# Queueing weight splits behind a tile's norm chain and behind the splits of probabilities in a two-layer hybrid attention trunk

## The chip, the core and the metric

The kernel runs on one core of one Trainium2 chip. The metric is the device time of one execution in microseconds. A core has a matrix engine (TensorE, PE in the profile, with its weight loads as PEld), three engines for elementwise work (VectorE: DVE, ScalarE: ACT, GpSimd: POOL) and a queue that issues the loads (SyncE: SP). Each engine has its own queue, whose order is fixed when the program is built; semaphores order the engines among each other. The program keeps eight PSUM tiles (banks) of 128 x 512 f32, which TensorE writes.

## What is computed

Two layers over 512 tokens of width 1024. Each layer normalizes, projects once, runs eight heads of forgetting attention and eight of dilated windows in parallel, and closes with an output projection and a gated input embedding:

```python
u = rms_norm(h, norm_g)
z = u @ w_in                                   # q, k, v, gate of both kinds, and the forget gate
qa = rms_norm(heads(qa, N_HEADS_FOX), qk_g[0]) # per head, also ka, qb, kb; qb and kb get a partial rope
oa = forgetting_attention(qa, ka, va, log_f) * silu(ga)
ob = dilated_attention(qb, kb, vb) * silu(gb)
h = h + concat([oa, ob]) @ w_out
gate = sigmoid(rms_norm(h, ple_norm_g) @ w_ple_gate)
return h + (p_i @ w_ple) * gate
```

## The kernel before

**Precision.** Every matmul is made of three: each operand is split into a high part, rounded to the fast matmul type (`hi`), and the remainder (`lo`), and hi x hi, hi x lo and lo x hi are added in PSUM (`mm3`). The split of a slab is an ACT copy into `hi` (L157 for weights, L616 for probabilities) and a DVE subtraction into `lo` (L158, L617).

**Weights.** Each pair of heads needs four slabs: `q` in three pieces of 1152, 1152 and 768 columns, and `g` (the gate) of 1024. They are loaded by SP into three raw buffers and split into five slots. `W.pump(n)` splits the next n slabs if a slot is free (`ready`); a slot is free when its earlier slab's last matmul is written. A load for a slab is issued when the third slab ahead of it has been split.

**The steps.** Each layer walks over eight pairs p (0 to 3 dilated, 4 to 7 forgetting). In step p TensorE projects the four token tiles t of pair p (`pj`), computes the scores of pair p-1 (`att_s`), applies the probabilities of pair p-2 to the values head by head (`att_pv`), computes the gate of pair p (`gate_mm`), and transposes the probabilities of pair p-1 (`att_tp` for 64 x 64 blocks into four banks `psS`, `att_tp2` for two whole 128 x 128 blocks per head into one bank `psA`) and the queries and keys of pair p (`att_z`). The matmuls stand in the order of the program (`InOrder`). The other engines' order is made by a scheduler from data dependences and the program's order, so that an instruction that is ready early may be put ahead of one that is written before it.

**The norm chain** of tile t is `evac_proj_a` and `evac_proj_b`: a square on ACT (L431), a reduce and a scaling on DVE (L433, L434), a power on POOL (`f`, L436), the product z on DVE (L449), and for dilated pairs a partial rope (L454 to L457; on DVE for t=3, on POOL otherwise). The value part goes to `V2` (L442, L443). z is the last reader of the projection's bank. There are two banks `psA`; tiles t=0 to 3, the gate and the whole blocks take them in turn.

**The gate** is evacuated by `gate_evac`: a product on DVE that frees the bank (L471), a tanh on ACT (L472), a second product on DVE (L473).

**Probabilities.** `att_pt(j, ...)` splits head j's transposed probabilities into `PT` (hi and lo, 11 blocks each): the two whole blocks into blocks 1 and 2, the rest into 3 to 10. Block 0 is zero. `PT` serves one head at a time, so head 1's split waits until head 0's value matmuls have read it. `att_pv` ends with an ACT copy (`ob`, L633), a DVE sum (L634) and a POOL product with the gate (L636) for each head.

Step p begins with six of eight slices of tile 0, `att_pv` of head 0, `att_pt` of head 1, `W.pump(2)`, the rest of tile 0, three slices of tile 1, `att_pv` of head 1, and then the norm chain of tile 0 (L738 to L746). Two further slabs are pumped after the gate's matmuls (L761).

Of the kernel before, what the change touches and what calls it, by code (L numbers as in the profile page):

```python
# [9 lines left out]
F32 = mybir.dt.float32  # L10
F32R = mybir.dt.float32r
I32 = mybir.dt.int32
AF = mybir.ActivationFunctionType
ALU = mybir.AluOpType
# [3 lines left out]
P = 128  # L18
# [7 lines left out]
HD = 64  # L26
# [175 lines left out]
def trunk(tc, ap):  # L202
# [3 lines left out]
    with ctx:  # L206
# [32 lines left out]
        W = Weights(nc, wp, rp, specs)  # L239
# [28 lines left out]
        QQ = [cp.tile([P, S], F32R, name=f"QQ{i}") for i in range(2)]  # L268
        KK = [cp.tile([P, S], F32R, name=f"KK{i}") for i in range(2)]
        CB = cp.tile([P, S], F32R, name="CB")  # L270
        PT = [cp.tile([P, 11, P], F32R, name=f"PT{i}") for i in range(2)]
        for l in range(DEPTH):
            W.own[("pt", l)] = (QQ, KK)
        C2 = cp.tile([40, S], F32R, name="C2")
# [80 lines left out]
        def rope_tables(l):  # L355
            for kind in range(2):
                for half in range(2):
# [6 lines left out]
                    def g(h):  # L364
# [3 lines left out]
                    V.tensor_tensor(out(Sg), b(nsinT if half == 0 else sinT), g(1 - half),  # L368
                                    op=ALU.mult)


        def square_acc(h, d, E=V):
            if d == 0:
# [52 lines left out]
        def evac_proj_a(l, p, t, ps, st):  # L426
            if p == 0:
                sq = U[t][:, :2 * P].rearrange("p (h d) -> p h d", h=4)
            else:
                sq = tp.tile([P, 4, HD], F32, tag="sq", name="sq", bufs=1)  # L430
            A.activation(sq, ps[:, :2 * P].rearrange("p (h d) -> p h d", h=4), AF.Square)  # L431
            ms = sp.tile([P, 4], F32, tag="ms", name="ms")
            V.tensor_reduce(ms, sq, axis=AX.X, op=ALU.add)  # L433
            V.tensor_scalar(ms, ms, 1.0 / HD, st["E"][:, t:t + 1], op0=ALU.mult, op1=ALU.add)  # L434
            f = sp.tile([P, 4], F32, tag="f", name="f")
            G.tensor_tensor(f, ms, mhalf.to_broadcast([P, 4]), op=ALU.pow)  # L436
            if p == 0:
                V.scalar_tensor_tensor(fx[:, t], ps[:, QW:QW0], st["r"][:, t:t + 1], bf[:, l],
                                       op0=ALU.mult, op1=ALU.add)
            v2 = V2[p % 2]  # L440
            vps = ps[:, 2 * P:QW].rearrange("p (h d) -> p h d", h=2)
            A.activation(v2[:, t, :, 0:HD], vps, AF.Copy, scale=st["r"][:, t:t + 1])  # L442
            V.scalar_tensor_tensor(v2[:, t, :, HD:P], vps, st["r"][:, t:t + 1],  # L443
                                   v2[:, t, :, 0:HD].bitcast(F32), op0=ALU.mult, op1=ALU.subtract)
            return f

        def evac_proj_b(l, p, t, ps, f):
            z = zp.tile([P, 4, HD], F32, tag="z", name="z")
            V.tensor_tensor(z, ps[:, :2 * P].rearrange("p (h d) -> p h d", h=4),  # L449
                            f[:, :, None].to_broadcast([P, 4, HD]), op=ALU.mult)  # L450
            if p < NDIL:
                E = V if t == NT - 1 or p == 0 else G
                tm = sp.tile([P, 4, 16], F32, tag="tm", name="tm", bufs=1)
                E.tensor_tensor(tm[:, :, 0:8], z[:, :, 8:16], Sg[:, t, :, 0:8], op=ALU.mult)  # L454
                E.tensor_tensor(tm[:, :, 8:16], z[:, :, 0:8], Sg[:, t, :, 8:16], op=ALU.mult)
                E.tensor_tensor(z[:, :, 0:16], z[:, :, 0:16], Cg[:, t], op=ALU.mult)
                E.tensor_tensor(z[:, :, 0:16], z[:, :, 0:16], tm, op=ALU.add)  # L457
            return z


# [7 lines left out]
        def gate_evac(p, ps):  # L468
            gt = U[5 + p % 2]
            th = tp.tile([P, S], F32, tag="sqh", name="sqh")  # L470
            V.tensor_tensor(gt, ps, Rh, op=ALU.mult)  # L471
            A.activation(th, gt, AF.Tanh)  # L472
            V.scalar_tensor_tensor(gt, th, 1.0, gt, op0=ALU.add, op1=ALU.mult)  # L473


        def log_forget(l):
# [40 lines left out]
        def flip(dst, src):  # L517
            for h in range(2):
                T.transpose(dst[h], src[HALF[h]], ident[HALF[h], HALF[h]])
# [77 lines left out]
        def att_tp(banks):  # L597

            for j, blocks in enumerate(att_blocks()):
                for i in range(8):  # L600
                    flip([x[:, i * 64:i * 64 + 64] for x in banks[j]], blocks[i + 2])

        def att_tp2(b0):

            for j, blocks in enumerate(att_blocks()):
                for i in range(2):
                    T.transpose(b0[:, (2 * j + i) * P:(2 * j + i + 1) * P], blocks[i], ident)

        def att_pt(j, banks, b0, pt=PT):
            parts = [(b0[:, 2 * j * P:2 * (j + 1) * P].rearrange("p (a b) -> p a b", a=2),  # L610
                      [x[:, 1:3] for x in pt])]
            for h in range(2):
                parts.append((banks[j][h].rearrange("p (a c) -> p a c", a=8),
                              [x[:, 3:11, HALF[h]] for x in pt]))
            for src, (hi, lo) in parts:
                A.activation(hi, src, AF.Copy)  # L616
                V.tensor_tensor(lo, src, hi.bitcast(F32), op=ALU.subtract)  # L617

        def att_pv(a, j, pt=PT):
            ps = ptile(psS, "psS")  # L620
            v2 = V2[a % 2]
            for i in range(2):
                for kt in range(NT):
                    q0 = min(kt, 2)
                    if kt < 3:
                        rhs = pt[i][:, KOFF[kt]:KOFF[kt] + NT - kt]
                    else:
                        rhs = pt[i][:, 0::10]
                    T.matmul(ps[:, q0 * P:], v2[:, kt, j], rhs, start=(kt == 0 and i == 0),
                             stop=(kt == NT - 1 and i == 1))  # L630
            b = slice(64 * j, 64 * j + 64)
            tm = tp.tile([HD, S], F32, tag="ob", name="ob")
            A.activation(tm, ps[64:128], AF.Copy)  # L633
            V.tensor_tensor(U[7][b], ps[0:64], tm, op=ALU.add)  # L634
            E = V if a == NPAIR - 1 else G
            E.tensor_tensor(U[7][b], U[7][b], U[5 + a % 2][b], op=ALU.mult)  # L636
# [29 lines left out]
        for l in range(DEPTH):  # L666
# [51 lines left out]
            replicate(rh, psS, "psS")  # L718
            if l == 0:
                scale_columns()  # L720
            gate_evac(0, gps)

            for p in range(1, NPAIR):
# [11 lines left out]
                else:  # L737
                    pj(p, 0, 0, 6)  # L738
                    att_pv(b, 0)
                    att_pt(1, tps, tpb)  # L740
                    W.pump(2)
                    pj(p, 0, 6, NK)
                    pj(p, 1, 0, 3)
                    att_pv(b, 1)
# [11 lines left out]
                if p == NDIL:  # L756
# [1 line left out]
                    bias_rows(p)  # L758
                gps = ptile(psA, "psA")
                gate_mm(l, p, u, gps, 0, NK)  # L760
                W.pump(2)  # L761
                tps = [pair(psS, "psS") for _ in range(2)]
                att_tp(tps)
                pqk = att_z(zt(p))
                tpb = ptile(psA, "psA")
                att_tp2(tpb)
                gate_evac(p, gps)
                att_pt(0, tps, tpb)
                att_qk(l, p, pqk)

            a, b = NPAIR - 1, NPAIR - 2
            part(0, 0, 5)
            att_pv(b, 0)
            att_pt(1, tps, tpb)
            W.pump()
            part(0, 5, 6)
            part(1, 0, 3)
# [2 lines left out]
            part(1, 3, 5)  # L780
            att_o(b, oo)
            att_s(a)
            PT1 = [x.rearrange("p k s -> p (k s)")[:, :11 * P].rearrange("p (a b) -> p a b", a=11)
                   for x in u]
            for x in PT1:
                G.memset(x[:, 0].bitcast(F32), 0.0)
# [8 lines left out]
            att_tp(tps)  # L795
            att_tp2(tpb)
            part(2, 5, 7)
            att_pt(0, tps, tpb)
            att_pt(1, tps, tpb, PT1)
            att_pv(a, 0)  # L800
            att_pv(a, 1, PT1)
            W.pump()
# [134 lines left out]
```

## Time and profile before

| what | value |
|---|---|
| time, median of 3 runs | 735.4 us (732.83 to 736.61) |
| the profiled execution, time | 735.51 us |
| its span, from the first to the last instruction | 733.7 us |
| mean granted TensorE clock | 0.99 |
| HBM read, written | 60.49 MB, 4.19 MB |
| DMA, mean over the span | 89 GB/s |

The span is what the trace shows; 1.8 us of the execution lie around it. The profile gives each engine's busy time, the waits between engines, and a timeline. A row of the timeline is: start, duration (both us), engine, line, operation, what it writes and reads with shapes, and in brackets how long the engine had stood idle and which instruction ended that. Rows with x2 or more join equal neighbours. A matmul's shown end is modelled: neighbours overlap, and their starts tell their pace. An instruction of DVE or ACT is shown to begin some 0.08 us before the one ahead of it ends. Lines are those of the kernel before; the changed kernel's stand 9 to 27 lines further down (L436 there is L445, L449 is L458, L471 is L482, L616 and L617 are L621 and L622, L633 to L636 are L652 to L655).

### The profile page before, as it was taken

To read this page: it belongs to the slowest core of one execution; us is meant where nothing else is said; L and a number is where in the kernel's file an instruction comes from. 1 tells how busy PE (TensorE), PEld (TensorE's weight loads), DVE (VectorE), ACT (ScalarE), POOL (GpSimd) and SP (SyncE) were. 2 spreads that over 40 slices of the span, in tenths; PEclk is the share of its full clock that TensorE was granted. 3 is DMA by queue.
4 is the path that set the end of the run, shared out by engine and by line. 5 is a ranking of instruction groups with operands and counts; after the bars stand their busy time and mean duration, and the time that the engine had idled before them with its cause. 6 is when DMAs were issued, how large, how long until landed. Compare 5 with 4: busy or idle time off the path is not lost.

```text
span 733.7 us, 12192 instructions
## 1 busy us (share of the span) xinstructions
PE 707.4 (96%) x4424; PEld 624.1 (85%) x4424; DVE 505.8 (69%) x1242; ACT 387.8 (53%) x823; POOL 212.7 (29%) x354
## 2 busy tenths in 40 slices
PE   9998998999999999999999998989999999999997
PEld 8998897989888788888899898989888897888886
DVE  7877677786857757838738777676767767586533
ACT  8674556474654655625525646465555646573310
POOL 7362634325142330000004534524232332300000
PEclk9999999999999999999999999999999999999999
DMA  8503123030303214515323113030402203344211
GB/s 292 176 30 116 36 80 88 29 116 2 116 2 115 70 62 142 188 46 186 116 85 116 56 61 115 2 115 2 116 19 98 87 30 116 88 143 144 87 43 44
DMA packets 23948, 65.54 MB, mean 89 GB/s; under 512 B 4816, under 2 KB 6096, under 8 KB 23888
## 3 DMA queue, kind: packets, MB, share of 16 engines
q1 hardware_dynamic: 22576, 64.68, 27.6%
q8 instruction: 35, 0.57, 0.3%
q10 hardware_dynamic: 1312, 0.08, 0.1%
q14 instruction: 25, 0.20, 0.1%
HBM read 60.49 MB, written 4.19 MB: 88 GB/s over the span
## 4 chain that ended last, share of the span: by engine, by line
PE 53%; DVE 20%; ACT 11%; POOL 9%; issue 5%; ACTq 1%; DMA 1%; DVEq 0%; POOLq 0%
PE psA L88 34%; PE psS L88 14%; POOL f L436 6%; DVE wlo L158 6%; ACT U L588 5%; PE psM L88 4%; DVE PT L617 3%; ACT whi L157 2%; DVE ms L434 2%; POOL U L636 1%; DVE ms L433 1%; ACTq L512 1%; DVE z L449 1%; DVE U L634 1%; DVE V L443 1%
## 5 line engine op out<-in xcount | busy, mean ns | idle before, releaser
L157 ACT ACTIVATE whi<-raw 128x1024 fp32r<-128x1024 f32 (+3 forms) x105 | 104.2, 1014 | 93.5 <-PE psA L88 51.3
L158 DVE TENSOR_TENSOR wlo<-raw,whi 128x1024 fp32r<-128x1024 f32 (+3 forms) x105 | 122.1, 1174 | 20.6 <-ACT whi L157 19.9
L88 PE MATMUL psA<-whi,X 128*128 128x384 f32 (+1 forms) x480 | 133.2, 346 | 2.5 <-DVE U L471 2.1
L88 PE MATMUL psA<-whi,Y 128*128 128x384 f32 (+1 forms) x480 | 131.4, 344 | 2.8 <-DVE U L471 2.3
L88 PE MATMUL psA<-Y,whi 128*128 128x512 f32 (+1 forms) x320 | 97.7, 389 | 2.1 <-DVE U L471 1.6
L88 PE MATMUL psA<-X,whi 128*128 128x512 f32 x304 | 95.9, 396 | 1.1 <-DVE U L471 1.0
L88 PEld LDWEIGHTS psA<-whi,X 128*128 128x128 f32 x480 | 89.3, 191 | 5.9 <-DVE U L471 3.1
L436 POOL TENSOR_TENSOR f<-ms,mhalf 128x4 f32<-128x4 f32 x64 | 68.6, 1072 | 88.6 <-DVE ms L434 78.8
L88 PEld LDWEIGHTS psA<-whi,Y 128*128 128x128 f32 x480 | 88.7, 190 | 5.6 <-DVE U L471 3.0
L588 ACT ACTIVATE U<-U,mx 128x512 f32<-128x512 f32 (+3 forms) x128 | 70.6, 553 | 36.3 <-DVE mx L586 36.2
L636 POOL TENSOR_TENSOR U<-U,U 64x512 f32<-64x512 f32 x28 | 36.0, 1286 | 179.7 <-DVE U L634 179.4
L88 PE MATMUL psA<-wlo,X 128*128 128x384 f32 (+1 forms) x240 | 82.0, 342 | 0.2 <-DVE wlo L158 0.2
L88 PE MATMUL psA<-wlo,Y 128*128 128x384 f32 (+1 forms) x240 | 81.7, 340 | 0.0
L590 POOL TENSOR_SCALAR U<-U,sm 128x512 f32<-128x512 f32 (+3 forms) x128 | 66.1, 537 | 26.2 <-DVE sm L589 25.4
L88 PEld LDWEIGHTS psA<-Y,whi 128*128 128x128 f32 x320 | 59.2, 190 | 15.3 <-DVE U L471 1.9
L88 PEld LDWEIGHTS psA<-X,whi 128*128 128x128 f32 x304 | 56.4, 188 | 14.7 <-DVE U L471 1.2
L88 PE MATMUL psA<-Y,wlo 128*128 128x512 f32 (+1 forms) x160 | 62.0, 387 | 0.0
L449 DVE TENSOR_TENSOR z<-psA,f 128x256 f32<-128x256 f32 x60 | 25.5, 424 | 50.7 <-POOL f L436 50.7
L88 PE MATMUL psA<-X,wlo 128*128 128x512 f32 x152 | 59.9, 394 | 0.0
L397 POOL TENSOR_TENSOR r<-m,mhalf 128x4 f32<-128x4 f32 x4 | 4.7, 1186 | 160.5 <-DVE m L396 160.5
L88 PEld LDWEIGHTS psA<-wlo,X 128*128 128x128 f32 x240 | 46.0, 192 | 0.6 <-DVE wlo L158 0.6
L88 PE MATMUL psS<-PT,V 128*128 128x512 f32 x240 | 45.0, 327 | 0.7 <-DVE X L617 0.3
(191 smaller groups left out, 1288.1 us busy)
## 6 DMA issues: line engine op xcount, KB each, us to landing
raw<-in_wq_dram SPq DMA_DIRECT2D x28, 576.0 KB, 4.0
raw<-in_wg_dram SPq DMA_DIRECT2D x16, 512.0 KB, 3.6
raw<-in_wo_dram SPq DMA_DIRECT2D x16, 512.0 KB, 4.0
raw<-in_wpg_dram SPq DMA_DIRECT2D x16, 512.0 KB, 3.4
raw<-in_wq_dram SPq DMA_DIRECT2D x14, 384.0 KB, 4.0
U<-in_xT_dram SPq DMA_DIRECT2D x16, 256.0 KB, 4.5
raw<-in_wple_dram SPq DMA_DIRECT2D x4, 512.0 KB, 3.6
hs<-U SPq DMA_DIRECT2D x8, 256.0 KB, 3.3
```

Source lines behind the costliest of these rows:

```text
L88: return self.tc.keep_in_program_order(self.eng.matmul(*a, **k))
L157: self.nc.scalar.activation(hi, r, AF.Copy)
L158: eng.tensor_tensor(lo, r, hi.bitcast(F32), op=ALU.subtract)
L433: V.tensor_reduce(ms, sq, axis=AX.X, op=ALU.add)
L434: V.tensor_scalar(ms, ms, 1.0 / HD, st["E"][:, t:t + 1], op0=ALU.mult, op1=ALU.add)
L436: G.tensor_tensor(f, ms, mhalf.to_broadcast([P, 4]), op=ALU.pow)
L443: V.scalar_tensor_tensor(v2[:, t, :, HD:P], vps, st["r"][:, t:t + 1], v2[:, t, :, 0:HD].bitcast(F32), op0=ALU.mult, op1=ALU.subtract)
L449: V.tensor_tensor(z, ps[:, :2 * P].rearrange("p (h d) -> p h d", h=4), f[:, :, None].to_broadcast([P, 4, HD]), op=ALU.mult)
L588: A.activation(seg, seg, AF.Exp, bias=mx, scale=-1.0, accum_out=sm)
L590: G.tensor_scalar(seg, seg, sm, 1.0, op0=ALU.mult, op1=ALU.mult)
L617: V.tensor_tensor(lo, src, hi.bitcast(F32), op=ALU.subtract)
L636: E.tensor_tensor(U[7][b], U[7][b], U[5 + a % 2][b], op=ALU.mult)
```

## The change

Three things change; the arithmetic is the same.

1. `behind("A", "V")` makes each instruction traced within it queue on its engine behind the last recorded one (`last`): the latest of the value copy, the gate's first product, z or its rope on DVE, and the probability splits. It is put around three calls of `W.pump`: after the gate's matmuls, where one slab is split in place of two; a new one after the whole blocks' split; and the one of two slabs after head 1's probabilities.
2. The whole blocks of both heads are split in one step (`att_pt2`), into blocks 9 to 12 of a `PT` of 13; `att_pv` reads them from there.
3. The gate's second product is written after `att_qk`.

```diff
-        PT = [cp.tile([P, 11, P], F32R, name=f"PT{i}") for i in range(2)]
+        PT = [cp.tile([P, 13, P], F32R, name=f"PT{i}") for i in range(2)]
...
+        last = {}
+
+        def behind(*engines):
+
+            st = ExitStack()
+            for e in engines:
+                st.enter_context(tc.issue_after(last[e].ins))
+            return st
...
-            A.activation(v2[:, t, :, 0:HD], vps, AF.Copy, scale=st["r"][:, t:t + 1])
+            last["A"] = A.activation(v2[:, t, :, 0:HD], vps, AF.Copy, scale=st["r"][:, t:t + 1])
...
-                E.tensor_tensor(z[:, :, 0:16], z[:, :, 0:16], tm, op=ALU.add)
+                done = E.tensor_tensor(z[:, :, 0:16], z[:, :, 0:16], tm, op=ALU.add)
+                if E is V:
+                    last["V"] = done
...
-            V.scalar_tensor_tensor(gt, th, 1.0, gt, op0=ALU.add, op1=ALU.mult)
+            return lambda: V.scalar_tensor_tensor(gt, th, 1.0, gt, op0=ALU.add, op1=ALU.mult)
...
+        def halve(hi, lo, src):
+            last["A"] = A.activation(hi, src, AF.Copy)
+            last["V"] = V.tensor_tensor(lo, src, hi.bitcast(F32), op=ALU.subtract)
+
+        def att_pt2(b0, j=None, pt=PT):
+
+            jj = range(2) if j is None else range(j, j + 1)
+            for x0, x1 in ((jj[0], jj[-1] + 1),):
+                src = b0[:, 2 * P * x0:2 * P * x1].rearrange("p (a b) -> p a b", b=P)
+                halve(*[x[:, 9 + 2 * x0:9 + 2 * x1] for x in pt], src)
+
+        def att_pt(j, banks, pt=PT):
             for h in range(2):
+                halve(*[x[:, 1:9, HALF[h]] for x in pt],
+                      banks[j][h].rearrange("p (a c) -> p a c", a=8))
...
-                    if kt < 3:
+                    if kt < 2:
                         rhs = pt[i][:, KOFF[kt]:KOFF[kt] + NT - kt]
+                    elif kt == 2:
+                        rhs = pt[i][:, 8:10 + 2 * j:1 + 2 * j]
                     else:
-                        rhs = pt[i][:, 0::10]
+                        rhs = pt[i][:, 0:11 + 2 * j:10 + 2 * j]
...
-                    att_pt(1, tps, tpb)
-                    W.pump(2)
+                    att_pt(1, tps)
+                    with behind("A", "V"):
+                        W.pump(2)
...
-                W.pump(2)
+                with behind("A", "V"):
+                    W.pump()
...
-                gate_evac(p, gps)
-                att_pt(0, tps, tpb)
+                rest = gate_evac(p, gps)
+                att_pt(0, tps)
+                att_pt2(tpb)
+                with behind("A", "V"):
+                    W.pump()
                 att_qk(l, p, pqk)
+                rest()
```

How the built order moves, at two places. First DVE at the end of step p=2 of the first layer, from the norm chain of tile 3 to the gate's evacuation; before:

```order
L158 TENSOR_TENSOR wlo<-raw,whi 128x1152
L433 TENSOR_REDUCE ms<-sq 128x4
L443 SCALAR_TENSOR_TENSOR V_115<-psA,r,V_115 128x2x64
L434 TENSOR_SCALAR ms<-ms,E 128x4
L158 TENSOR_TENSOR wlo<-raw,whi 128x768
L449 TENSOR_TENSOR z<-psA,f 128x256
L158 TENSOR_TENSOR wlo<-raw,whi 128x1024
L454 TENSOR_TENSOR tm<-z,Sg 128x4x8
L455 TENSOR_TENSOR tm<-z,Sg 128x4x8
L456 TENSOR_TENSOR z<-z,Cg 128x4x16
L457 TENSOR_TENSOR z<-z,tm 128x4x16
L471 TENSOR_TENSOR U_93<-psA,Rh 128x512
```

and of the change:

```order
L442 TENSOR_REDUCE ms<-sq 128x4
L452 SCALAR_TENSOR_TENSOR V_115<-psA,r,V_115 128x2x64
L443 TENSOR_SCALAR ms<-ms,E 128x4
L458 TENSOR_TENSOR z<-psA,f 128x256
L463 TENSOR_TENSOR tm<-z,Sg 128x4x8
L464 TENSOR_TENSOR tm<-z,Sg 128x4x8
L465 TENSOR_TENSOR z<-z,Cg 128x4x16
L466 TENSOR_TENSOR z<-z,tm 128x4x16
L158 TENSOR_TENSOR wlo<-raw,whi 128x1152
L482 TENSOR_TENSOR U_93<-psA,Rh 128x512
```

Three splits that stood within the chain are now one behind it. The other slabs (768, 1024, 1152) stand later: the next rows are DVE's in step p=3, from the second head's probabilities to z of tile 0, in the change (before, no split stood there):

```order
L622 TENSOR_TENSOR PT_123<-psS,PT_122 128x8x64 x2
L653 TENSOR_TENSOR U_95<-psS,ob 64x512
L158 TENSOR_TENSOR wlo<-raw,whi 128x1024
L158 TENSOR_TENSOR wlo<-raw,whi 128x1152
L442 TENSOR_REDUCE ms<-sq 128x4
L653 TENSOR_TENSOR U_95<-psS,ob 64x512
L443 TENSOR_SCALAR ms<-ms,E 128x4
L452 SCALAR_TENSOR_TENSOR V_116<-psA,r,V_116 128x2x64
L458 TENSOR_TENSOR z<-psA,f 128x256
```

The second head's sum (second L653) also moved, from behind z to ahead of it. Last, POOL from the end of step p=3's scaled probabilities on (`f` is the power of the norm chain, `U_95` the head output times the gate); before:

```order
L590 TENSOR_SCALAR U_92<-U_92,sm 128x128
L436 TENSOR_TENSOR f<-ms,mhalf 128x4
L636 TENSOR_TENSOR U_95<-U_95,U_93 64x512
L436 TENSOR_TENSOR f<-ms,mhalf 128x4
L636 TENSOR_TENSOR U_95<-U_95,U_93 64x512
L436 TENSOR_TENSOR f<-ms,mhalf 128x4 x2
```

and of the change:

```order
L601 TENSOR_SCALAR U_89<-U_89,sm 128x128
L601 TENSOR_SCALAR U_92<-U_92,sm 128x128
L445 TENSOR_TENSOR f<-ms,mhalf 128x4
L655 TENSOR_TENSOR U_95<-U_95,U_93 64x512 x2
L445 TENSOR_TENSOR f<-ms,mhalf 128x4 x3
```

The first f is tile 3's of the step that ends. The next one is tile 0's: it stood between the two heads' products and now stands behind both. This holds in steps p=2 to 7 of both layers. On SP the loads of weights keep their order.

More of the change, by code (lines that the diff above doesn't have):

```diff
@@ L448, in evac_proj_b @@
             z = zp.tile([P, 4, HD], F32, tag="z", name="z")
-            V.tensor_tensor(z, ps[:, :2 * P].rearrange("p (h d) -> p h d", h=4),
-                            f[:, :, None].to_broadcast([P, 4, HD]), op=ALU.mult)
+            last["V"] = V.tensor_tensor(z, ps[:, :2 * P].rearrange("p (h d) -> p h d", h=4),
+                                        f[:, :, None].to_broadcast([P, 4, HD]), op=ALU.mult)
             if p < NDIL:
@@ L470, in gate_evac @@
             th = tp.tile([P, S], F32, tag="sqh", name="sqh")
-            V.tensor_tensor(gt, ps, Rh, op=ALU.mult)
+            last["V"] = V.tensor_tensor(gt, ps, Rh, op=ALU.mult)
             A.activation(th, gt, AF.Tanh)
-            V.scalar_tensor_tensor(gt, th, 1.0, gt, op0=ALU.add, op1=ALU.mult)
+            return lambda: V.scalar_tensor_tensor(gt, th, 1.0, gt, op0=ALU.add, op1=ALU.mult)
         def log_forget(l):
@@ L600, in att_tp @@
                 for i in range(8):
-                    flip([x[:, i * 64:i * 64 + 64] for x in banks[j]], blocks[i + 2])
+                    flip([x[:, i * 64:i * 64 + 64] for x in banks[j]], blocks[i])
         def att_tp2(b0):
@@ L606, in att_tp2 @@
                 for i in range(2):
[L607 to L611, printed above, removed]
-            for h in range(2):
[L613 to L617, printed above, removed]
+                    T.transpose(b0[:, (2 * j + i) * P:(2 * j + i + 1) * P], blocks[i + 8], ident)
+        def halve(hi, lo, src):
[7 more added lines that the diff above has]
+        def att_pt(j, banks, pt=PT):
+            for h in range(2):
+                halve(*[x[:, 1:9, HALF[h]] for x in pt],
+                      banks[j][h].rearrange("p (a c) -> p a c", a=8))
         def att_pv(a, j, pt=PT):
@@ L720, in trunk @@
                 scale_columns()
-            gate_evac(0, gps)
+            gate_evac(0, gps)()
             for p in range(1, NPAIR):
@@ L773, in trunk @@
             att_pv(b, 0)
-            att_pt(1, tps, tpb)
+            att_pt(1, tps)
             W.pump()
@@ L782, in trunk @@
             att_s(a)
-            PT1 = [x.rearrange("p k s -> p (k s)")[:, :11 * P].rearrange("p (a b) -> p a b", a=11)
+            PT1 = [x.rearrange("p k s -> p (k s)")[:, :13 * P].rearrange("p (a b) -> p a b", a=13)
                    for x in u]
@@ L797, in trunk @@
             part(2, 5, 7)
-            att_pt(0, tps, tpb)
-            att_pt(1, tps, tpb, PT1)
+            att_pt(0, tps)
+            att_pt2(tpb, 0)
+            att_pt(1, tps, PT1)
+            att_pt2(tpb, 1, PT1)
             att_pv(a, 0)
```

## The prediction

> **What bounds the kernel now.** I read the page's busy times first, then who waits for whom on TensorE, then the timeline around each wait.
>
> ```profile
> span 733.7 us, 12192 instructions
> ...
> PE 707.4 (96%) x4424; PEld 624.1 (85%) x4424; DVE 505.8 (69%) x1242; ACT 387.8 (53%) x823; POOL 212.7 (29%) x354
> ```
>
> TensorE is the bound: it is idle for only 26 us of 733.7, so an edit on ACT, DVE or POOL counts only where TensorE waits for it. The view of waits, for the matmuls (PE) and the weight loads (PEld), gives total, number and longest:
>
> ```profile
> PE psM L91 <- DVE z L457: 10.9, 6, 2.3
> PE psA L88 <- DVE U L471: 7.0, 8, 1.6
> PE psA L88 <- DVE PT L617: 0.7, 4, 0.2
> ...
> PEld psM L91 <- DVE z L457: 11.7, 6, 2.4
> PEld psA L88 <- DVE U L471: 9.1, 9, 1.9
> PEld psA L88 <- DVE PT L617: 3.3, 7, 0.5
> ```
>
> Three waits at the end of a step, and all three are the ones the change aims at: the transposes of z of the last token tile wait for its rope (L457), the next projection waits for the gate's bank (L471), and the one after for the bank of the whole blocks (L617). They sum to 18.6 us for PE and 24.1 us for PEld. PE's figure is too small, since a matmul is shown for 0.34 us but follows its neighbour at 0.175 us (rows 167.28 and 167.45 below), so each of the 18 waits hides some 0.17 us: 21.6. I take **23 us**, between this and PEld's.
>
> A stall has a second price. The view of busy time by stretches, cut in windows of 3.41 us (columns: length, busy time of PE, PEld, DVE, ACT, POOL, granted clock, DMA):
>
> ```profile
> 60.32:63.73 3.41, 3.41 (x16) 3.35 (x13) 3.41 (x6) 2.33 (x6) 0.00 (x0) 0.50 0.78 201
> ...
> 91.04:94.45 3.41, 1.92 (x25) 1.71 (x20) 3.35 (x7) 2.17 (x3) 0.00 (x0) 1.00 0.78 234
> 251.47:254.88 3.41, 1.80 (x34) 1.45 (x31) 3.41 (x5) 0.86 (x2) 0.00 (x0) 1.00 0.66 193
> 483.57:486.99 3.41, 1.53 (x13) 1.46 (x14) 3.35 (x7) 2.11 (x3) 0.00 (x0) 1.00 0.75 229
> ...
> 486.99:490.40 3.41, 3.41 (x13) 3.41 (x12) 3.41 (x8) 2.31 (x7) 0.00 (x0) 0.50 0.63 232
> ```
>
> Four windows between the start and the end run at clock 0.50, from 60.3, 125.2, 254.9 and 487.0 us (first and last shown). Each follows a window in which PE was busy for 1.80 us or less; a window with 1.92 was not followed by one. In the last, 13 matmuls of 0.175 us fill a window that would hold 3.41 us of them: 3.41 - 2.28 = 1.15 us lost. Four make **4.6 us**, and they go if their stalls go.
>
> **What the change removes.** The end of step p=3, in the order of time:
>
> ```profile
> 117.28 1.89 ACT L157 ACTIVATE whi<-raw 128x1152 fp32r<-128x1152 f32 x2
> 120.45 0.95 DVE L158 TENSOR_TENSOR wlo<-raw,whi 128x768 fp32r<-128x768 f32 x1
> 120.63 1.65 POOL L436 TENSOR_TENSOR f<-ms,mhalf 128x4 f32<-128x4 f32 x1 [2.25 <-DVE ms L434]
> 122.75 1.23 DVE L158 TENSOR_TENSOR wlo<-raw,whi 128x1024 fp32r<-128x1024 f32 x1
> 124.80 0.34 PE L91 MATMUL psM<-cst,z 64*128 64x64 f32 x4 [2.16 <-DVE z L457]
> 125.20 0.69 DVE L471 TENSOR_TENSOR U<-psA,Rh 128x512 f32<-128x512 f32 x1
> ```
>
> The norm chain (square, reduce, f, z, rope) stands behind two whi on ACT (1.89), and on DVE and POOL behind three wlo. With one split, queued behind the chain, the square starts 1.8 us earlier, f no longer takes 1.65 for 1.01, and z's rope no longer follows the 1.23 us split: about 1.8 + 0.6 + 1.2 = 3.6 us earlier, against a wait of 2.16. The gate's evacuation then starts when the gate's matmuls end, not at 125.20, and both heads' whole blocks leave their bank before the next step needs it. I cost all three waits at nothing afterwards: **-23 - 4.6 = -27.6 us**. A margin of 1.4 us covers the first. The second split of the two (768 columns) moves to after the probabilities of the first head; its wlo is due when the step's first projection reaches its seventh slice, behind the first head's eight value matmuls, and I estimate that it ends about 0.9 us before that; if it came late, each step would wait by the excess, at most the 0.95 us of the split itself. Merging two whole-block splits into one saves 0.15 us of DVE in 14 places; DVE is not the bound there, so nothing. The loads keep their order on SP and are three deep; a split that comes some us later finds its data, since a load lands 4 us after its issue and is asked for three splits ahead.
>
> **What it adds.** The other two splits of a step (1024 and 1152 columns, the second `W.pump(2)`) used to stand in the step before. They now stand behind the second head's probabilities, in front of the next tile's norm chain. ACT has both whi ahead of the square of tile t=0; DVE has both wlo ahead of its reduce and of the second head's sum (L634, L653 after). POOL's queue shows what follows: both gate products (L636, L655 after) now stand ahead of f of t=0, which stood between them. z of t=0 frees the bank of `psA` that tile t=2's projection writes, and there are two such banks. So **the projection of t=2 now waits for the second head's whole tail**. Its pieces, in step p=5 of before:
>
> ```profile
> 165.41 0.67 DVE L634 TENSOR_TENSOR U<-psS,ob 64x512 f32<-64x512 f32 x1
> 166.00 1.44 PE L88 MATMUL psS<-PT,V 128*128 128x512 f32 x8
> 166.16 1.29 POOL L636 TENSOR_TENSOR U<-U,U 64x512 f32<-64x512 f32 x1 [12.05 <-DVE U L634]
> 166.45 1.03 DVE L434 TENSOR_SCALAR ms<-ms,E 128x4 f32<-128x4 f32 x1
> 167.28 0.34 PE L88 MATMUL psA<-whi,X 128*128 128x384 f32 x1
> 167.45 0.34 PE L88 MATMUL psA<-wlo,X 128*128 128x384 f32 x1
> 167.48 0.60 ACT L633 ACTIVATE ob<-psS 64x512 f32<-64x512 f32 x1
> 167.56 1.01 POOL L436 TENSOR_TENSOR f<-ms,mhalf 128x4 f32<-128x4 f32 x1
> 168.60 0.42 DVE L449 TENSOR_TENSOR z<-psA,f 128x256 f32<-128x256 f32 x1 [0.78 <-POOL f L436]
> 169.88 1.28 POOL L636 TENSOR_TENSOR U<-U,U 64x512 f32<-64x512 f32 x1 [1.32 <-DVE U L634]
> ```
>
> In after the rows follow one another: value matmuls end, ob 0.60, sum 0.67, product 1.28, f 1.01, z 0.42, with 0.35 of handover (0.04 to 0.14 each): 4.35 us. TensorE has in that time 15 matmuls of t=1, from 167.28 on, 15 x 0.175 = 2.63, of which 0.16 passes before 167.44: cover 2.45. So the wait is at least **1.9 us**, in each of steps p=2 to 7 of both layers: 12 times, 22.8 us at the least.
>
> The splits make it longer. Let Z be the start of the first head's eight value matmuls. DVE takes the second head's probabilities from Z+1.4 (their buffer is being read before), 1.2 us for two, and the first head's sum until Z+3.25. Now the two splits' durations (busy us, then mean ns of one):
>
> ```profile
> L158 DVE TENSOR_TENSOR wlo<-raw,whi 128x1024 fp32r<-128x1024 f32 x52 | 63.0, 1221 | 2.4 <-ACT whi L157 1.7
> L158 DVE TENSOR_TENSOR wlo<-raw,whi 128x1152 fp32r<-128x1152 f32 x28 | 37.9, 1355 | 17.6 <-ACT whi L157 17.6
> ```
>
> And from the timelines of DVE and POOL, early in the program:
>
> ```profile
> 9.11 0.69 DVE L378 TENSOR_TENSOR acc<-acc,sqh 128x512 f32<-128x512 f32 x1
> 9.35 0.57 POOL L295 TENSOR_TENSOR ang<-ang,cosT 128x32 f32<-128x32 f32 x1
> 9.73 0.74 DVE L384 SCALAR_TENSOR_TENSOR X<-U,gn,X 128x512 fp32r<-128x512 f32 x1
> ...
> 51.21 0.57 DVE L485 TENSOR_TENSOR lf<-lf,lf 128x32 f32<-128x32 f32 x1
> ```
>
> POOL's f at 120.63 took 1.65, not 1.01, and began its work when the split of 120.45 ended; a POOL product of 1.29 us held DVE's ms of 166.45 until it ended; a 32-element tensor-tensor on DVE took 0.57 at 51.21 beside POOL's scalings. So DVE operations that read two SBUF operands and POOL operations shut each other out. At 9.35 POOL got in between two such DVE operations that followed each other directly: it ended at 9.92, just behind the one of 9.11. In after the first product asks at Z+3.4, just behind the 1024 split's start at Z+3.25. It waits for that split's end, Z+4.35, runs 1.28 to Z+5.6, and the 1152 split, shut out, ends at Z+6.75. Then reduce (0.3), sum until Z+7.7, product Z+7.85 to 9.13, f to 10.2, z to 10.65. TensorE is ready for t=2 at Z + 1.29 + 6 x 0.175 + 9 x 0.175 + 1.28 + 2.63 = Z+7.83. The wait is **2.85 us**. Bounds: 1.9 where nothing collides, 2.85 with the collision; I take 2.85, since the row of 9.35 is the only one in which POOL asks between two DVE operations.
>
> The Trainium skill (SBUF — State Buffer, Who interferes with whom) says that a VectorE instruction with two SBUF inputs and a GpSimd one that reads SBUF take turns at one port, whole instructions, by order of issue. By that the product, issued ahead of the second split, goes first, and the sum is the one I take.
>
> A wait of 2.85 leaves a window of 3.41 us with too little work unless the window's edge cuts it so that neither part is over some 1.75 us (3.41 - 1.80, and the 0.17 that PE's shown ends hide): an edge in 0.65 of 3.41 us, one in five. So 10 of 12 are followed by a half-clock window: 10 x 1.15 = 11.5 us.
>
> **Sum.** 12 x 2.85 = 34.2, + 11.5, - 27.6 = +18.1. The profiled execution took 735.5 us (span 733.7 and 1.8 around it), the median of the runs shown is 735.4: **753.5 us**.
>
> **Rivals.**
> - DVE keeps the port for both splits. The first product then runs Z+5.7 to 7.0, the second to 8.3, z ends at 9.8: a wait of 2.0, 12 x 2.0 = 24, and 7 windows by the same count of edges (8): 24 + 8 - 27.6 = +4.5, **740 us**. For it: DVE's next operation stands ready in its queue. Against: the row of 9.35.
> - Faster than before. One mechanism: the new wait stays at its least, 1.9, and the half-clock windows miss it. 22.8 - 27.6 = -4.8, **730.5 us**. It decides the sign below a mean of 2.3 us a wait including the clock. For it: a stall of 1.69 us at 91 us had no half-clock window behind it. Against: the 251.47 window had one with 1.80 busy.
> - The change brings its saving and no new wait, because t=2's projection does not in fact depend on the product: -27.6, **708 us**. Against: POOL's rows in this trace stand in the order of its queue, and f is behind.
> - The clock. The windows above were followed by half clock after stalls under 2.5 us. If the new waits, which sit elsewhere in the step, did not trip it: 34.2 - 27.6 = +6.6, **742 us**. The Trainium skill (TensorE: Matmul & The Clock Gate, Why this matters for your kernels) asks only that gaps between bursts stay below some 3 us; by that rule the waits here would be free of it. This trace disagrees, with 2.16 us of wait at 124.80 and half clock from 125.2.
>
> **How the numbers follow.** Forecast 0.50 (its own range 747 to 760), DVE first 0.20, no clock loss 0.08, least wait 0.15, no new wait 0.07. The range 729 to 760 takes in all but the last and the tails. About 0.5% (3.7 us) is what a measurement can tell here. Faster by more: 0.07 and most of the least wait, 0.18. Slower by more: forecast, the no-clock case and a little under half of DVE first, 0.66. Within: 0.16.
>
> **What would show it.** In the profile after: no wait of psM for z's rope (10.9 before), none of psA for L471's successor; a new wait of psA for z (L458), 12 times, 2.7 us shown, some 0.17 less than its cost; POOL's f of t=0 directly behind two products; the first product lengthened beside a 1024 split, or the 1152 split beside it; some ten windows at 0.50 and a mean clock near 0.97. It is wrong if t=2's projection does not wait, or if the old waits stay; if the waits are near 2.0, the port was taken the other way.

## The result, and the profile after

The changed kernel is slower, and by more than predicted:

| | before | after |
|---|---|---|
| time, median of 4 runs | 734.62 us (732.83 to 736.61) | 764.48 us (761.52 to 764.67) |
| ratio, with its 95% interval | | 1.0396 (1.0358 to 1.0435) |
| profiled execution: time, span | 735.51, 733.7 us | 761.52, 759.5 us |
| mean granted TensorE clock in the runs | 0.99 | 0.978 in the profiled one, 0.972 to 0.974 in the others |

The page after: span, and busy times by engine.

```profile
span 759.5 us, 12111 instructions
...
PE 711.9 (94%) x4424; PEld 630.7 (83%) x4424; DVE 510.1 (67%) x1228; ACT 383.6 (51%) x809; POOL 212.4 (28%) x354
```

TensorE has the same 4424 matmuls and is shown busy for 4.5 us more, so some of them ran slower; and it is idle for 47.6 us against 26.3. The view of waits after (total, number, longest) says where:

```profile
PE psA L88 <- DVE z L458: 40.0, 12, 4.5
...
PEld psA L88 <- issue: 43.5, 12, 4.8
```

The three waits of before (psM for z's rope, psA for the gate, psA for the whole blocks) are gone, every one. In their place stands one wait, 12 times: the one that was predicted, at the projection of tile 2, for z of tile 0. The weight loads show it as "issue", because they are queued behind the matmul that waits.

I measure stalls by starts, since a matmul's shown end is modelled: each matmul's distance to the next, less the median distance of its shape. What stands above the median sums to 80.4 us before and 105.8 after, some 25 more, and the profiled executions differ by 26.0. Of the 105.8, the 12 stalls are 41.9 (of the 80.4, 19.2 are stalls over 0.8 us): nine of 3.17 to 3.57, one of 2.60, and two, in step p=5 of each layer, of 4.65 and 4.63.

One step in the order of time, p=6 of the first layer (the first head's value matmuls start at Z = 203.79), with rows of p=5 ahead of it (there Z = 166.30) and one of p=7 behind:

```profile
160.72 0.68 DVE L514 TENSOR_TENSOR C<-c,C 8x512 fp32r<-8x512 f32 x1 [0.70 <-ACT C L513]
161.44 0.69 DVE L482 TENSOR_TENSOR U<-psA,Rh 128x512 f32<-128x512 f32 x1
...
171.32 0.67 DVE L653 TENSOR_TENSOR U<-psS,ob 64x512 f32<-64x512 f32 x1
179.85 0.41 PE L88 MATMUL psA<-whi,X 128*128 128x384 f32 x1 [4.49 <-DVE z L458]
...
206.12 1.05 ACT L157 ACTIVATE whi<-raw 128x1024 fp32r<-128x1024 f32 x1
206.42 0.67 DVE L653 TENSOR_TENSOR U<-psS,ob 64x512 f32<-64x512 f32 x1
207.18 1.29 POOL L655 TENSOR_TENSOR U<-U,U 64x512 f32<-64x512 f32 x1 [9.96 <-DVE U L653]
207.20 2.35 DVE L158 TENSOR_TENSOR wlo<-raw,whi 128x1024 fp32r<-128x1024 f32 x1
209.48 1.34 DVE L158 TENSOR_TENSOR wlo<-raw,whi 128x1152 fp32r<-128x1152 f32 x1
211.18 0.69 DVE L653 TENSOR_TENSOR U<-psS,ob 64x512 f32<-64x512 f32 x1
212.01 1.26 POOL L655 TENSOR_TENSOR U<-U,U 64x512 f32<-64x512 f32 x1 [3.54 <-DVE U L653]
213.35 1.01 POOL L445 TENSOR_TENSOR f<-ms,mhalf 128x4 f32<-128x4 f32 x1
214.39 0.42 DVE L458 TENSOR_TENSOR z<-psA,f 128x256 f32<-128x256 f32 x1 [2.01 <-POOL f L445]
214.97 0.66 PE L88 MATMUL psA<-whi,X 128*128 128x384 f32 x1 [3.19 <-DVE z L458]
...
242.08 2.38 POOL L655 TENSOR_TENSOR U<-U,U 64x512 f32<-64x512 f32 x1 [10.00 <-DVE U L653]
```

Read from 206.42 down, this is the predicted chain: first sum, first product beside the 1024 split, the 1152 split, second sum, second product, f, z, matmul. The collision is there, but the other way round: the product starts 0.02 us **ahead** of the split, and it is the first split that is held, 2.35 us in place of 1.22. The matmul starts at Z+11.18. The product is ahead of the first split in nine of the 12 steps. In the other three it got in between the two splits, as predicted: at 242.08 above, at the same place of the second layer, and in p=4 of the first:

```profile
134.57 1.21 DVE L158 TENSOR_TENSOR wlo<-raw,whi 128x1024 fp32r<-128x1024 f32 x1
134.72 2.21 POOL L655 TENSOR_TENSOR U<-U,U 64x512 f32<-64x512 f32 x1 [11.52 <-DVE U L653]
```

The stall in p=4 is 3.35 us, the same as in p=6, so it isn't the order at this place that makes the wait longer than predicted.

The clock, in windows of 3.41 us (columns as before), around two of the stalls:

```profile
210.97:214.39 3.42, 0.81 (x5) 0.49 (x3) 1.35 (x4) 1.06 (x3) 2.27 (x2) 1.00 0.75 244
214.39:217.80 3.41, 2.83 (x9) 2.87 (x10) 2.17 (x6) 0.21 (x1) 1.01 (x1) 0.50 0.02 6
...
245.68:249.10 3.42, 0.99 (x6) 0.67 (x4) 1.36 (x4) 1.05 (x3) 2.27 (x2) 1.00 0.57 193
249.10:252.51 3.41, 2.83 (x16) 2.86 (x17) 2.17 (x6) 0.22 (x1) 1.01 (x1) 1.00 0.01 2
```

Behind the first, half clock: 9 matmuls start in 2.83 us. Behind the second, whose first window is as empty, 16 start in 2.83 us at full clock. In the profiled execution nine of the 12 stalls have a half-clock window behind them; the slowed matmuls (some 90) lose 13.4 us by starts, 1.36 to 1.55 us a window.

### The profile page after: what moved, and what is told of

Read it like the earlier page. It is cut to its first block, busy times and chain, and to the rows that moved or that the text cites. A ratio compares the mean times of both kernels' runs of the same rounds, so it can differ in the third digit from the quotient of the medians.

```text
span 759.5 us, 12111 instructions
## 1 busy us (share of the span) xinstructions
PE 711.9 (94%) x4424; PEld 630.7 (83%) x4424; DVE 510.1 (67%) x1228; ACT 383.6 (51%) x809; POOL 212.4 (28%) x354
## 4 chain that ended last, share of the span: by engine, by line
PE 71%; DVE 10%; ACT 8%; issue 5%; POOL 5%; ACTq 1%; DMA 0%; SPq 0%; POOLq 0%; DVEq 0%
PE psA L88 49%; PE psS L88 15%; PE psM L88 4%; DVE wlo L158 4%; POOL f L445 3%; ACT PT L621 2%; POOL U L655 2%; ACT whi L157 2%; ACT U L599 2%; PE psS L91 2%; DVE U L653 1%; PE psM L91 1%; DVE z L458 1%; ACT ob L652 1%; PE psA L91 1%
## 5 line engine op out<-in xcount | busy, mean ns | idle before, releaser
L88 PE MATMUL psA<-whi,X 128*128 128x384 f32 (+1 forms) x480 | 137.6, 355 | 20.5 <-DVE z L458 20.5
L88 PE MATMUL psA<-whi,Y 128*128 128x384 f32 (+1 forms) x480 | 135.1, 351 | 19.5 <-DVE z L458 19.5
L158 DVE TENSOR_TENSOR wlo<-raw,whi 128x1024 fp32r<-128x1024 f32 (+3 forms) x105 | 135.0, 1296 | 12.7 <-ACT whi L157 12.0
L88 PEld LDWEIGHTS psA<-whi,X 128*128 128x128 f32 x480 | 92.8, 199 | 23.7 <-issue 22.2
L88 PEld LDWEIGHTS psA<-whi,Y 128*128 128x128 f32 x480 | 91.3, 196 | 22.3 <-issue 21.3
L655 POOL TENSOR_TENSOR U<-U,U 64x512 f32<-64x512 f32 x28 | 38.9, 1388 | 197.9 <-DVE U L653 197.9
L445 POOL TENSOR_TENSOR f<-ms,mhalf 128x4 f32<-128x4 f32 x64 | 64.7, 1011 | 97.1 <-DVE ms L443 87.3
L88 PE MATMUL psA<-wlo,X 128*128 128x384 f32 (+1 forms) x240 | 84.5, 352 | 0.5 <-DVE wlo L158 0.5
L88 PEld LDWEIGHTS psA<-Y,whi 128*128 128x128 f32 x320 | 58.4, 188 | 13.2 <-DVE sqh L860 1.2
L440 ACT ACTIVATE sq<-psA 128x256 f32<-128x256 f32 x56 | 21.3, 381 | 82.6 <-PE psA L88 76.3
L442 DVE TENSOR_REDUCE ms<-sq 128x4 f32<-128x256 f32 x56 | 23.3, 416 | 47.4 <-ACT sq L440 46.4
```

The lines of the kernel that those rows point to most:

```text
L88: return self.tc.keep_in_program_order(self.eng.matmul(*a, **k))
L158: eng.tensor_tensor(lo, r, hi.bitcast(F32), op=ALU.subtract)
```

## The experiments

Diffs are against the changed kernel, but for the two runs that start from the kernel before. "Stalls" are sums by starts, as above (41.9 us in the changed kernel), of those over 0.8 us.

**1 and 2. The tail of the second head, piece by piece.** Does POOL's queue make the wait, or do the splits alone? First only the product moves behind f; then the sum on DVE too.

```diff
-                    att_pv(b, 1)
+                    gate2 = att_pv(b, 1, late=True)   # run 1: the product; run 2: sum and product
                     pj(p, 1, 3, NK)
                     ev(p, 0)
+                    with behind("G"):                 # behind tile 0's f
+                        gate2()
```

> The changed kernel, but the second head's product with the gate queues on POOL behind tile 0's f (DVE's queue stays as it is). Theory (POOL's queue puts the product of 1.28 us into the chain that frees the bank): z of tile 0 comes about 1.3 us earlier, each of the 12 waits falls from 3.35 us (4.6 in p=5) to about 2.1, so 12 x 1.3 = 15.5 us less; with a few half-clock windows fewer, 744 to 750 us. Rival (the two splits alone set z of tile 0, the product is hidden behind the second head's sum): no change, 764 us.

> As the run before, and the second head's sum on DVE is also written behind tile 0's norm chain, so only the two splits stay ahead of that chain. Theory: the chain loses the sum of 0.69 us as well; each wait is about 1.4 us, a stall that most half-clock windows no longer follow: 728 to 740 us. If the waits came from the two splits alone, 764 us again; if from the tail alone, no wait is left and the time is near 711.

Measured 745.50 us (ratio to before 1.0126, 1.0087 to 1.0164) and 728.65 us (0.9910, 0.9882 to 0.9937). The row of the wait, in the first and in the second:

```profile
PE psA L88 <- DVE z L458: 26.1, 12, 3.3
```

```profile
PE psA L88 <- DVE z L458: 19.2, 12, 2.8
```

The stalls fall to 28.0 and 21.1 us: the product is worth 13.9 (1.16 a step), the sum 6.9 (0.58), and both times lie in their ranges. The queue theory holds, with its size. What stays I put down to the splits themselves, which run 3 moves. One stall of 12 has a half-clock window behind it in the second, seven in the first.

**3, 10 and 5. The splits behind tile 0's chain.** If the wait comes from what stands ahead of that chain, then moving the pair of splits behind it should leave the gain alone. The three runs make one more move each (run 10 is run 3 with att_o moved, run 5 is run 10 with the gate's split moved).

```diff
                     att_pt(1, tps)
-                    with behind("A", "V"):
-                        W.pump(2)
...
                     ev(p, 0)
+                    with behind("A", "V"):            # run 3
+                        W.pump(2)
-                    att_o(b, oo)
                 ev(p, 1)
+                if p > 1:
+                    att_o(b, oo)                      # runs 10 and 5
...
-                with behind("A", "V"):
-                    W.pump()
...
                 rest = gate_evac(p, gps)
+                with behind("V"):                     # run 5
+                    W.pump()
```

> The changed kernel, but the pair of splits (1024 and 1152 columns) is written behind tile 0's norm chain and queues behind its z. Theory: the reduce of tile 0 is again ahead of the second head's sum and f ahead of its product, as before the change; z of tile 0 is ready near Z+6.2 us (Z the start of the first head's value matmuls) where TensorE asks at Z+7.8; the 12 waits (41.9 us) and the half-clock windows behind them (9, some 12.5 us) go, but for some 0.7 us in p=5: 709 to 715 us, faster than both kernels. Rival (with the pair of splits later, the next tile's chain or the next wait takes over): 730 us or more.

Measured 727.55 us (0.9895, 0.9868 to 0.9922): the wait for tile 0 is gone, but the time is some 12 us over the expected range. Waits of run 3:

```profile
PE psA L88 <- DVE z L458: 6.8, 8, 1.2
PE psA L88 <- DVE U L482: 6.3, 10, 1.2
```

The first line reads like the old wait and is another: it is tile 3's projection, waiting for z of tile 1. DVE's timeline, in step p=4 of the second layer, shows why:

```profile
494.07 0.69 DVE L659 TENSOR_TENSOR X<-U,X 128x512 fp32r<-128x512 f32 x1 [1.84 <-ACT X L658]
494.68 0.41 DVE L442 TENSOR_REDUCE ms<-sq 128x4 f32<-128x256 f32 x1
```

The split of both heads' output (L659, in `att_o`) waits 1.84 us for the second head's product (through ACT's L658), and tile 1's reduce is queued behind it.

> The third run with the sum of both heads behind tile 1's chain, the first of the two moves of the fifth. Theory: the waits for z of tile 1 go (6.8 us in the third run, 6.3 us for the gate's bank stay): 719 to 722 us. Rival (the place of the split ahead of the gate's product is what both waits come from): 726 us or more.

> The splits after tile 0's z as in the third run, with two more moves: the sum of both heads (att_o) is written behind tile 1's norm chain, which it held in that run while it waited for POOL; and the split after the gate's matmuls queues behind the gate's first product and no longer ahead of it. Theory (each wait left in the third run, 6.8 us for z of tile 1 and 6.3 us for the gate's bank, came from what stood ahead in DVE's queue): both go, 709 to 716 us. Rival (DVE, busy 506 of 726 us, is nearly full in each step, so that a wait that is removed comes back at another place): 722 us or more.

Measured 707.27 us (0.9598, 0.9577 to 0.9619) and **704.90 us** (0.9586, 0.9558 to 0.9614). The expectation for run 10 was wrong by 12 us: I took the two waits of run 3 for two causes, but the waits for the gate's bank went with the others, though nothing at their place was changed. I take them for the lateness of tile 1, carried through DVE to the end of the step; I haven't followed it row by row. Run 5 is 4 us below its range. Whether the move of the gate's split adds anything can't be told: the intervals overlap. The page of run 5:

```profile
span 703.4 us, 12122 instructions
...
PE 696.1 (99%) x4424; PEld 619.0 (88%) x4424; DVE 511.0 (73%) x1228; ACT 384.0 (55%) x809; POOL 225.2 (32%) x354
```

TensorE is idle for 7 us, no stall of over 0.8 us is left in the steps, and the clock is 1.00. The three waits that the change removes are absent in run 5 too, and it is 4.1% faster than the kernel before.

**4 and 9. Which edit makes the wait.** Run 4 leaves out one `behind`, at the pair of splits; run 9 puts that one `behind` into the kernel before and nothing else.

```diff
                     att_pt(1, tps)
-                    with behind("A", "V"):            # run 4 takes this away, run 9 adds it to before
-                        W.pump(2)
+                    W.pump(2)
```

> The changed kernel, but the pair of splits after head 1's probabilities is not forced behind them (the other two forced places and the joint split of the whole blocks stay). The order then puts both splits ahead of head 1's probabilities and f of tile 0 ahead of the second head's product. Theory: no wait of the bank for z of tile 0; instead DVE ends head 1's lo probabilities some 2.5 us later and TensorE waits for them, about 1.5 us a step: 725 to 740 us. Rival (it is the delay of the splits as such that costs, or the other two forced places): 755 us or more.

> The kernel before, with the pair of splits after head 1's probabilities forced behind them and nothing else of the change. Theory (this edit alone makes the new wait): 12 waits of 3.3 us for z of tile 0 with their half-clock windows, and of the old waits what the two splits that stay at the end of a step leave, at most 10 us: 760 to 772 us. Rival (the new wait needs the other forced places, or the longer queue at the step's end): 740 us or less.

Measured 726.36 us (0.9875, 0.9844 to 0.9906) and 775.69 us (1.0523, 1.0498 to 1.0548). The waits of run 4 and of run 9:

```profile
PE psS L88 <- DVE PT L622: 6.2, 8, 0.9
PE psA L88 <- DVE z L458: 5.4, 4, 1.9
```

```profile
PE psA L88 <- DVE z L458: 39.6, 12, 3.5
PE psA L88 <- DVE U L480: 3.3, 3, 1.9
```

That one `behind` makes the whole wait by itself, and makes it in a kernel that has nothing else of the change: the 12 waits are 3.3 to 3.6 us there. Without it the splits stand ahead of head 1's probabilities, and TensorE waits a little for those. Four waits for z of tile 0 are left in run 4, against the expectation: two of 2.1 us in p=2 and two of 0.9 in p=5. There the built order still has the 1152 split between head 1's probabilities and tile 0's reduce. Run 9 is 4 us over its range: 11 stalls have half-clock windows behind them, five of them two in a row, and its mean clock is 0.965.

**6 and 12. The half clock.** Matmuls whose result nobody reads fill the wait, wholly or in part.

```diff
                 ev(p, 1)
+                if p > 1:
+                    fill = ptile(psM, "psM")
+                    for i in range(13):               # run 12: 6
+                        T.matmul(fill, tri[:, 0:P], tri[:, P:], start=True, stop=True)
                 pj(p, 2)
```

> The changed kernel with 13 matmuls of 512 columns more, in steps p=2 to 7, ahead of tile 2's projection; their result is read by nobody. They take 13 x 0.23 = 3.0 us, less than the wait of 3.35 us (4.6 in p=5), so they add no time if the wait is made elsewhere; they keep TensorE busy. Theory (the half-clock windows come from the stall): windows behind the waits go but perhaps in p=5, 9 to 11 x 1.4 us = 12 to 15 us less, 749 to 753 us. Rival (the half clock has another cause): 764 us; if the wait were TensorE's own: 764 + 36 = 800 us.

> The sixth run with 6 matmuls in the wait, not 13: 1.4 us of it filled, some 1.95 us of stall left (3.2 in p=5). Theory (a half-clock window needs a stall of over 2 us, as none of the shorter ones in the runs so far had one behind it): windows in p=5 alone, 749 to 753 us as with 13. Rival (any wait of this kind brings it): 760 us or more.

Measured 748.60 us (748.29 to 749.06) for the first, 0.4 below its range. From the grouped view and the windows of run 6:

```profile
L88 PE MATMUL psM<-tri 128*128 128x512 f32 x156 | 37.6, 391 | 0.0
```

```profile
205.00:208.41 3.41, 3.16 (x15) 2.37 (x14) 1.35 (x4) 1.27 (x3) 2.30 (x2) 1.00 0.55 173
208.41:211.82 3.41, 3.41 (x21) 3.41 (x20) 1.30 (x5) 0.00 (x0) 1.01 (x1) 1.00 0.03 5
```

TensorE is shown busy for 37.6 us more (156 matmuls, some 36 us by starts) and the kernel is 15.9 us faster than the changed one by the medians, 13.2 by the profiled executions (748.29 against 761.52), as much as the nine windows cost there (13.4): the fill takes the time in which it stood still, and no half-clock window is left between 40 and 660 us. The chain that frees the bank is untouched, so the half clock is what the difference is, and it comes from the stall that the matmuls fill.

Run 12 missed: 756.79 us (752.88 to 761.61), and its four runs differ by 9 us. Windows of its steps p=3 and p=6:

```profile
105.20:108.61 3.41, 1.68 (x10) 1.71 (x11) 1.77 (x5) 1.27 (x3) 2.64 (x7) 1.00 0.31 127
108.61:112.03 3.42, 3.42 (x22) 3.09 (x22) 0.64 (x2) 0.63 (x2) 1.98 (x5) 1.00 0.00 0
...
209.02:212.43 3.41, 1.57 (x8) 1.10 (x7) 1.38 (x5) 1.27 (x3) 2.19 (x2) 1.00 0.47 156
212.43:215.84 3.41, 3.41 (x13) 3.41 (x12) 1.07 (x4) 0.00 (x0) 1.01 (x1) 0.50 0.00 0
```

Stalls of 1.97 and 1.99 us; the second has a half-clock window behind it (11 matmuls start there, 20 in the other window; the views' x13 and x22 count those too that began ahead of the edge). In its profiled execution four stalls of 1.97 to 2.01 have one and two of the same length don't. The threshold of 2 us that I expected is no threshold but lies in a range with both outcomes. Its ground was wrong already: in the kernel before, a stall of 1.77 us at 252.63 has the half-clock window of 254.9 behind it.

**7. The joint split alone**, in the kernel before (blocks 9 to 12 of `PT`, `att_pt2`).

> The kernel before, with the joint split of the whole blocks alone; nothing is forced behind anything. Theory (by the waits of before, the whole blocks' bank costs 0.7 us on the matmuls and 3.3 us on the weight loads): 731 to 735 us. Rival (the joint split brings the change's gain): 725 us or less.

Measured 734.06 us (0.9985, 0.9966 to 1.0004): no change that can be told. Its waits:

```profile
PE psA L88 <- DVE U L471: 10.7, 9, 2.4
PE psM L91 <- DVE z L457: 10.6, 6, 2.3
```

The wait for the whole blocks' bank is gone, and the gate's wait has grown from 7.0 to 10.7. So the gain of the change doesn't come from the joint split. I put it down to the splits that left the end of the step; no run moves the gate's second product alone.

**8. The products on DVE.**

```diff
-            E = V if a == NPAIR - 1 else G
+            E = V
```

> The changed kernel with both heads' products on DVE in place of POOL (some 0.65 us each there). Theory (POOL's product and the split of 1024 columns shut each other out, 1.1 us a step, and f waits behind the second product): the chain is sum, split, product, split, sum, reduce, product, f, z, and ends near Z+9.8 us against Z+11.2; each wait falls to about 2.1 us, 15 us less and a few windows fewer: 744 to 750 us. Rival (no exclusion; the split is slow for another reason): the two products add 1.3 us to DVE's chain and save 1.3 behind it, 760 us or more.

Measured 757.98 us (1.0307, 1.0271 to 1.0343), between the two. Grouped by shape, the 1024 split in the changed kernel and in run 8:

```profile
L158 DVE TENSOR_TENSOR wlo<-raw,whi 128x1024 fp32r<-128x1024 f32 x52 | 75.1, 1451 | 3.4 <-ACT whi L157 2.7
```

```profile
L158 DVE TENSOR_TENSOR wlo<-raw,whi 128x1024 fp32r<-128x1024 f32 x52 | 63.2, 1218 | 2.3 <-ACT whi L157 1.9
...
206.66 0.69 DVE L655 TENSOR_TENSOR U<-U,U 64x512 f32<-64x512 f32 x1
207.38 0.23 DVE L443 TENSOR_SCALAR ms<-ms,E 128x4 f32<-128x4 f32 x1
```

With no product on POOL no split is held: 1.22 us each, as before the change, so the exclusion is real. But the stalls fall only to 34.3 us, 2.4 to 2.6 in most steps where I expected 2.1, because the second product stands ahead of `ms` on DVE (the last two rows), which f needs; and stalls of that length still bring half clock behind ten of the 12 (16.2 us by starts).

**11. Step p=5.** Its stall was 1.3 us longer than the others. In the rows of p=5 the cumulative sums (L512, L514) stand ahead of the gate's product, which starts at 161.44. They move to step p=2:

```diff
-                if p == NDIL:
+                if p == 2:
                     cumulate()
+                if p == NDIL:
                     bias_rows(p)
```

> The changed kernel with the cumulative forget sums (two DVE operations ahead of the gate's product) at the end of step p=2, not p=4. Theory (those two operations make step p=5's wait 4.65 us long, against 3.35): the excess moves to p=3 and p=5 falls to 3.35; the time stays, 762 to 767 us. Rival (p=5 is long because it is the first step whose pair needs bias rows): p=5 stays at 4.6.

Measured 760.59 us (757.51 to 762.95; 1.0323, 1.0287 to 1.0358), 1.4 below its range. Step p=5 falls to 3.33 and 3.30 us. But the edit moved more than the sums: the built order now has the four loads of bias rows, which ACT issues (L523), in step p=2 too. The row of run 11, and two of the changed kernel:

```profile
89.83 2.60 ACTq L523 DMA_DIRECT2D CB<-C  x4
```

```profile
160.72 3.24 ACTq L523 DMA_DIRECT2D CB<-C  x4
164.01 0.63 ACT L483 ACTIVATE sqh<-U 128x512 f32<-128x512 f32 x1 [3.32 <-issue]
```

In the changed kernel the gate's tanh (L483) and the splits of probabilities behind it stand in ACT's queue behind these loads: the tanh starts 1.9 us after the end of the gate's product (162.13), where in p=6 it follows by 0.04 us. So run 11 shows that the sums and the loads that read them make p=5 longer; it doesn't tell them apart, and the rival of the bias rows, for which these rows speak, stays open. The excess did not move to p=3, as I expected, but went: that stall is 2.62, shorter than 3.33. The timeline of run 11 at p=3:

```profile
99.79 1.21 DVE L158 TENSOR_TENSOR wlo<-raw,whi 128x1024 fp32r<-128x1024 f32 x1
99.94 3.48 POOL L655 TENSOR_TENSOR U<-U,U 64x512 f32<-64x512 f32 x1 [12.45 <-DVE U L653]
...
106.46 0.66 PE L88 MATMUL psA<-whi,X 128*128 128x384 f32 x1 [2.46 <-DVE z L458]
```

Here DVE, a little later than usual, no longer waits for `whi`; its split starts 0.15 us ahead of POOL's product, both splits run through, and the product ends 3.48 us after it started. That is the rival "DVE keeps the port", at 2.30 to 2.62 us of stall; it holds at three steps of this run and at none of the changed kernel.

## Why the prediction was right, and where it failed

- **What bounds the kernel, and what goes:** right. Three waits went and none is left; the forecast was 27.6 us, and some 29.3 went (see the sum below). One cover failed in part: the split of 768 columns does come late in step p=5, 0.9 us in both layers together.
- **The new wait:** right in place, cause and count. Runs 1, 2 and 9 show the cause, and run 5 that no new wait follows once it is gone. The rival in which the projection does not wait (708 us) was wrong of the change, but its price was about right: run 5 does without the wait and takes 704.9.
- **The size of the wait** is the step that failed: 12 x 2.85 = 34.2 us forecast, 41.9 measured. The sentence that failed first is that the first product "asks at Z+3.4, just behind the 1024 split's start at Z+3.25". I had left out ACT: the split needs its `whi`, which stands behind two splits of probabilities and `ob` there and ends at 207.17, so that it starts at Z+3.41, 0.02 us behind the product, and not ahead. In p=6 the pair of splits then ends at Z+7.03, not Z+6.75: half of that is the later start (Z+3.39, with the product), the other half that the product and the two splits take 3.64 us together, where I had 3.50. The reduce behind them takes 0.40 us, not 0.3, and z ends at Z+11.02, not Z+10.65. The matmul starts 0.16 us after that, a handover that I had put at nothing. TensorE was ready at Z+7.83, as forecast. Nine of the waits are so 0.3 to 0.7 longer, 4.4 us in all; the two of p=5 are 3.6 longer together, where I had taken all steps for alike (run 11); the one of 2.60 is 0.25 shorter. Together 7.7.
- **The port:** the row at 9.35, from which I took that POOL gets in between two DVE operations, was a fair reading: at 242.08 the product starts with the first split, ends 2.38 us later, and the second split is held. But it is one of three outcomes, and run 11 shows the one of the rival. By the Trainium skill (SBUF — State Buffer, Who interferes with whom) the two engines take turns by order of issue. 207.18 against 207.20 agrees with that, and 99.94 does not fit it unless both splits count as issued, since there the product asks 0.98 us ahead of the second split's start and still comes behind it.
- **The clock:** the count was about right, the price too low. Forecast were 10 windows of 1.15, 11.5 us; in the profiled execution there are 9, of 1.36 to 1.55, 13.4 us. I had taken the price from the 13 matmuls that the view counts in the window of 486.99, but two of these began ahead of it: 11 start there, and by starts it lost 1.46. The other three runs had a mean clock lower by some 0.005, which over 762 us is about 2 more such windows (0.005 x 762 / 0.5 / 3.41), an estimated 3 us: the profiled execution, 761.5, is the fastest of the four, and the median is 764.5. The Trainium skill (TensorE: Matmul & The Clock Gate, Why this matters for your kernels) asks only that gaps stay below some 3 us. Eleven of the 12 waits came out at 3.17 us and more, so the changed kernel does not test that. Runs 8 and 12 do: half clock came behind six of eight stalls of 2.4 to 2.6 us and behind four of six of 1.97 to 2.01. By these, waits of 2.85 would not have been free of it either.
- **Sum:** +18.1 was 34.2 + 11.5 - 27.6. Measured between the profiled executions: 41.9 + 13.4 - 29.3 = 26.0. The 29.3 is what the difference leaves for what went; by starts, stalls over 0.8 us are 19.2 of it and the slowed matmuls of four windows 6.2, and the other 3.9 would be shorter waits, less the 0.9 that the late split adds. The range ended at 760 because every wait was put at one value, and the largest bound that I gave for it was the one I chose.

## What to carry to other kernels

An edit that moves work behind something also puts it ahead of something: write down, for every engine whose queue it changes, which operation now stands behind the moved one, and follow that to a buffer that the bound engine waits for. Here the whole loss came from one call that splits two slabs ahead of a tile's norm chain; with that call (and one reader of POOL's product) behind the chain, the same change is worth 4%. And a time at which an operation "asks" needs every one of its inputs: the ACT copy that I left out made the split 0.16 us late, which changed who had the port and was a part of what the wait came out longer. The handover at the end of a chain, also 0.16 us here, is another part of each wait.

## What the runs showed of the hardware

- **Stalls and the half clock.** Over all profiles of this case, of stalls of TensorE between 40 and 660 us: none of 39 from 0.8 to 1.5 us has a half-clock window behind it, 1 of 18 from 1.5 to 1.95, 28 of 48 from 1.95 to 3.2, and 31 of 34 longer ones. The share of a window that PE works, which I used, does not decide it alone: the window at 245.68 above, with 0.99 us of work, was followed by full clock. What does is open.
- **Small differences of start decide who has a shared resource.** POOL's product of 1.29 us costs DVE's split 1.13 us when it starts 0.02 us ahead, costs the next split 1.1 us when they start together, and is itself held for 2.2 us when it starts 0.15 us behind (run 11). At 134.57 and 134.72 of the changed kernel the same lag of 0.15 us let the product in after the first split, so the lag alone does not tell; that is open too.
